# Query projections of two cross-attention layers as 2x2 block products in seven multiplications

## The chip, the core and the metric

The kernel runs on one core of one Trainium2 chip. The metric is the device time of one execution in microseconds (us), the median of several runs. A core has five engines with a queue each: PE (TensorE, the matrix engine), DVE (VectorE), ACT (ScalarE), POOL (GpSimd) and SP (SyncE, here only an issuer of transfers). They run side by side and wait for one another by semaphores.

## The reference

A trunk of two residual layers over 1024 tokens of width 1024, everything in fp32. Each layer has a mixer, a cross-attention into 256 memory tokens and an MLP, every one behind an RMS norm. The change touches the query product of the cross-attention, `h @ wq`, and what feeds it:

```python
def cross_attention(h, mem_n, wq, wkv, wo):
    q = (h @ wq).reshape(B, S, X_HEADS, X_HEAD_DIM)
    kv = (mem_n @ wkv).reshape(B, M, 2, X_HEADS, X_HEAD_DIM)
    s = jnp.einsum('bshd,bmhd->bhsm', q, kv[:, :, 0]).astype(jnp.float32) * X_HEAD_DIM ** -0.5
    p = jax.nn.softmax(s, axis=-1)
    o = jnp.einsum('bhsm,bmhd->bshd', p.astype(h.dtype), kv[:, :, 1]).reshape(B, S, D_MODEL)
    return o @ wo
...
        h = h + even_mixer(hn, ...)       # layer 0; odd_mixer in layer 1
        h = h + cross_attention(rms_norm(h, norm_xattn_g[l]), mem_n, xattn_wq[l], xattn_wkv[l], xattn_wo[l])
        h = h + sq_relu_mlp(rms_norm(h, norm_mlp_g[l]), mlp_w1[l], mlp_w2[l])
```

## The kernel before, in words

**Operands.** Every fp32 matrix is cut in two (`cut`, L72 and L73): ACT copies it to a rounded type (hi), and DVE subtracts that from the original (lo). A product is three matmul passes: hi by hi, lo by hi, hi by lo. Activations lie transposed, as tiles of 128 channels by 1024 tokens; most live in a pool of 44 slots of 128x1024. Weights stream through four raw buffers (`wr`) and two buffers each for hi and lo (`wh`, `wl`). `w_cut` cuts one unit ahead of its use.

**Two kinds of product.** `gemm` makes one 128x1024 output tile: 8 channel tiles by 3 passes by 2 halves, 48 matmuls of 128x512. `split_gemm` makes two output tiles by a 2x2 block product in seven multiplications instead of eight: 7 products of 12 matmuls of 128x512, 84 instead of 96. It needs weights as sums and differences of blocks (POOL, L149 to L153, in the tiles `wr` and `wt`), the operand in seven such combinations (`combine`, L247 to L250, four adds on DVE, and the class `Split`, groups 0 to 3), and it adds seven partial results: products 0 to 6 lie in banks `x`, `yz`, and `evac` takes each to one or two of the four output blocks, by an ACT copy first and by DVE adds then. Before, only the MLP uses it (m0a and m1a: first matrix, m0b and m1b: second).

**Stages.** By the names of the trace, in order: the even mixer; `X`, its output product with the residual add (`residual`, L815); `c0q`, eight query gemms (`query`, L877); the cross stage with `c0s` (scores, L904), `c0s_p` (softmax: reduce L908, four exponentials L913, row scaling L922), `c0tp` (transposes) with `c0pt` (their cut) and `c0po` (times the values); `c0o`, its output product; m0a, m0b. Then layer 1: the conv mixer, `cvo` in the place of `X`, c1q, c1s to c1po, c1o, m1a, m1b.

**Around the change.** `residual` is called for `X`, `cvo`, `c0o` and `c1o`. With `split=True` (before: `c0o` and `c1o` alone) each pair of output tiles is scaled, combined and cut into the seven parted tiles of the following `split_gemm`; the last pair's tiles are needed by that one at once. Its first pair of output tiles is therefore run with `first=True`: products 0 and 1 on the first three channel steps, then their last step, then products 3 and 2 likewise. The norm's row factors are made in two steps (`stage1`, `stage2`: a POOL power of 1.65 us, L320), which come as hooks between products. Keys and values were computed ahead into memory; `kv_get(c)` (L867) loads 2 tiles of 512 KB and cuts them, hi on ACT (L872) and lo on POOL (L873). `kv_get(0)` stands behind query 3; `score(0)` stands ahead of the last query gemm (`query(7)`), and `kv_get(1)` behind `score(1)`.

The order within each engine's queue is made by a scheduler that follows the order of the code by priority and the buffers that are free.

Of the kernel before, what the change touches and what calls it, by code (L numbers as in the profile page):

```python
# [40 lines left out]
def hybrid_trunk(ctx: ExitStack, tc: tile.TileContext, xT, memT, vecs, lams, rel, onehot, negrow, invcnt,  # L41
# [48 lines left out]
    for l in range(2):  # L90
        if l == 1:
            for j in range(KT):
                order += [(FLAT, conv_in[i * KT + j]) for i in (1, 2, 0)]
            order += [(FLAT, conv_out[n]) for n in range(KT)]
        order += [(FLAT, wq[l, n]) for n in range(KT)]
        order += [(FLAT, wo[l, n]) for n in range(KT)]
        order += [(FLAT, w1[l, 2 * p], w1[l, 2 * p + 1]) for p in range(4 * KT // 2)]
        order += [(FLAT, w2[l, c, 2 * p], w2[l, c, 2 * p + 1]) for c in range(4) for p in range(KT // 2)]
# [77 lines left out]
    class Act:  # L176
# [75 lines left out]
    def split_gemm(act, name, evac, hooks=None, first=False, tail=False):  # L252
# [16 lines left out]
        def out(i):  # L269
            for n, h in (TAIL_ADDS if tail else ADDS)[i]:  # L270
                evac(n, h, banks[(TAIL if tail else SPLIT)[i][2]], (n, h) not in seen)
                seen.add((n, h))

        for i in range(7):
            if i % 2 == 0:
                ws.append(w_next())
            for fn in (hooks or {}).get(i, ()):
                fn()
            if first and i < 4:
                if i % 2 == 1:  # L280
# [509 lines left out]
    while wait:  # L790
        tock()
    Y = Act()
    for i, _ in enumerate(fill_kv(1)):
        if i % YGAP == 0 and i // YGAP < KT:
            k = (0, 1, 2, 4, 5, 6, 7, 3)[i // YGAP]
            Y.t[k] = pair(f"Y{k}")
            cut(*Y.t[k], o_t[k] if k < 4 else y_t[k - 4])

# [16 lines left out]
    def residual(act, g_col, name, split=False):  # L815
# [4 lines left out]
        for n in range(KT):  # L820
# [10 lines left out]
            if split and n == KT - 1:  # L831
                w, ps = w_next(), psg(f"{name}_{n}")
                for h in range(2):
# [18 lines left out]
            if split and n % 2 == 1:  # L852
                tt, t4 = (slot(f"{name}_t{i}_{j}") for i in range(2))
                combine(r[0], r[1], tt, t4[:, :H])
                for g, raw in ((1, tt), (2, r[1]), (3, t4[:, :H])):
                    nx.group(g, j, raw)
            if split and n == KT - 1:
                nn.add(t[:, half(1)], 1, last=True)
            h_store(n, t, name)
        return nx, nn  # L860

    X, nrm = residual(Y, G_X[0], "X1")

    def cross(l, X, nrm, g_next, name):
        kvp = {}

        def kv_get(c):  # L867
            for cc, sh in ((c, (P, 4, M)), (2 + c, (P, 2, H))):
# [3 lines left out]
                nc.scalar.activation(kvp[cc][0], t, AF.Copy)  # L872
                nc.gpsimd.tensor_sub(kvp[cc][1], t, f32(kvp[cc][0]))  # L873

        rc = small.tile([P, KT], F32, tag="rc16", name=f"{name}_rc16")
        Q = Act()
        def query(n):  # L877
            ps = gemm(X, f"{name}q{n}", {5: nrm.stage1} if n == 0 else None)
            Q.t[n] = pair(f"{name}q{n}")
            cut(*Q.t[n], ps)  # L880
            if n == 1:
                nc.vector.tensor_scalar_mul(rc, nrm.rcol, 1.0 / 16.0)
            if n == 3:
                kv_get(0)

        for n in range(KT - 1):
            query(n)
        units = [(h, th) for h in range(4) for th in range(2)]
# [58 lines left out]
        n = len(units)  # L947
        score(0)
        query(KT - 1)
        norm_p(0)  # L950
        for u in range(n + 1):
            if u + 1 < n:
                score(u + 1)
                if u == 0:
                    kv_get(1)
            if u >= 1:
# [10 lines left out]
    def mlp(l, X, nrm, g_next, name):  # L967
# [57 lines left out]

        def merged(*hooks):
            return {i: [f for h in hooks for f in h.get(i, ())] for i in range(7)}


# [9 lines left out]

        rest, ahead = {4: [nrm.stage1], 6: [nrm.stage2]}, []  # L1040
        for p in range(2 * KT):
# [62 lines left out]
    def conv_mixer(X, nrm, g_next, name):  # L1104
        hooks = with_norm(nrm)
        Y = Act()
        for j in range(KT):
# [18 lines left out]
            nc.vector.tensor_mul(y, y, psb_)  # L1126
            Y.t[j] = pair(f"{nm}g")
            cut(*Y.t[j], y)
        return residual(Y, g_next, f"{name}o")

# [30 lines left out]
def _layout(inp):  # L1161
# [40 lines left out]
    g["conv_out"] = tiles(a["conv_w_out"][0])  # L1202
    g["wq"] = tiles(a["xattn_wq"])
    g["wkv"] = a["xattn_wkv"].reshape(2, 4, 2, P, 4, H).transpose(0, 4, 1, 3, 2, 5)
    g["wo"] = tiles(a["xattn_wo"])

    halves = [0, 2, 4, 6, 1, 3, 5, 7]
    g["w1"] = tiles(a["mlp_w1"])[..., halves, :]
    g["w2"] = tiles(a["mlp_w2"].reshape(2, 4, D, D))[..., halves, :]
    return {n: np.ascontiguousarray(v) for n, v in g.items()}  # L1210

# [17 lines left out]
```

## Time and profile before

| | before |
|---|---|
| median of 3 runs | 2615.15 us (2613.42 to 2619.64) |
| the profiled execution | 2622.43 us, span of the trace 2620.6 us |
| PE busy | 2541.0 us, 97% of the span |
| DVE, ACT, POOL busy | 1641.9 (63%), 1009.8 (39%), 694.4 us (26%) |
| mean granted PE clock | 0.99 |
| HBM | 249.91 MB read, 114.03 MB written, 139 GB/s |

The span is what the trace covers; the execution's own time is 1.8 us more. PE's ends are modelled, so a busy PE is one with matmuls queued without a gap. A matmul row's own duration (0.39 us) overlaps that of the next; the distance between starts is what one costs.

### The profile page before, as it was taken

The numbers are of one execution on the slowest core, as the hardware profiler recorded it, in microseconds if no ns is written. First come the engines' busy times: TensorE is split into PE (matmuls) and PEld (weight loads), VectorE is DVE, ScalarE is ACT, GpSimd is POOL, SyncE is SP. The second block draws the span as 40 slices with busy tenths as digits, with TensorE's granted clock in tenths as the row PEclk, the third lists the DMA queues.
The fourth block names the chain that finished last, engine by engine and source line by source line (L and its number), as shares of the span: only waits on it lengthen the run. The fifth ranks groups of instructions, "written<-read, shape, count | busy, mean of one in ns | idle before, by whom it ended". The sixth has DMA issues, their size and how long they took to land.

```text
span 2620.6 us, 29978 instructions
## 1 busy us (share of the span) xinstructions
PE 2541.0 (97%) x11618; PEld 2076.6 (79%) x11618; DVE 1641.9 (63%) x1846; ACT 1009.8 (39%) x1389; POOL 694.4 (26%) x417
## 2 busy tenths in 40 slices
PE   7999999999999999999999999999999999999997
PEld 5777778888878888777788888888887888777786
DVE  7777764325567778877773333323566777877875
ACT  4554564225443334433342111222443433433432
POOL 3222100200233334323352111111032333422334
PEclk9999999999999999999999999999999999999998
DMA  5101146311324445777742111422133344777752
GB/s 170 33 25 49 52 160 211 112 66 51 114 89 144 149 161 212 282 266 248 256 143 73 49 49 51 145 82 70 49 121 113 141 158 159 261 268 241 264 203 95
DMA packets 108430, 365.89 MB, mean 140 GB/s; under 512 B 12416, under 2 KB 14848, under 8 KB 108288
## 3 DMA queue, kind: packets, MB, share of 16 engines
q1 hardware_dynamic: 74880, 252.82, 28.7%
q10 hardware_dynamic: 33408, 111.16, 11.1%
q8 instruction: 91, 1.49, 0.2%
q14 instruction: 51, 0.42, 0.1%
HBM read 249.91 MB, written 114.03 MB: 139 GB/s over the span
## 4 chain that ended last, share of the span: by engine, by line
PE 81%; DVE 7%; issue 6%; DMA 3%; ACT 2%; SPq 0%; POOL 0%; DVEq 0%; ACTq 0%; POOLq 0%
PE m1a_x L265 7%; PE m0a_x L265 7%; PE m1a_yz L265 5%; PE m0a_yz L265 5%; PE m1b_x L265 5%; PE m0b_x L265 4%; PE m1b_yz L265 4%; PE cvo L189 3%; PE X L189 3%; PE c0o L189 3%; PE c1o L189 3%; PE m0b_yz L265 3%; PE c1q L189 3%; PE c0q L189 3%; PE qkv L189 3%
## 5 line engine op out<-in xcount | busy, mean ns | idle before, releaser
L72 ACT ACTIVATE wh<-wr 128x1024 fp32r<-128x1024 f32 (+1 forms) x310 | 301.0, 971 | 953.5 <-PE m0b_yz L265 154.9
L73 DVE TENSOR_TENSOR wl<-wr,wh 128x1024 fp32r<-128x1024 f32 (+1 forms) x310 | 361.5, 1166 | 210.6 <-ACT wh L72 209.8
L152 POOL TENSOR_TENSOR wr<-wr,wr 128x512 f32<-128x512 f32 x63 | 88.7, 1408 | 703.0 <-DVE wl L73 703.0
L73 DVE TENSOR_TENSOR wl<-wt,wh 128x1024 fp32r<-128x1024 f32 x64 | 135.7, 2120 | 4.8 <-ACT wh L72 4.6
L153 POOL TENSOR_TENSOR wr<-wr,wt 128x512 f32<-128x512 f32 x63 | 125.8, 1997 | 0.0
L150 POOL TENSOR_TENSOR wt<-wr,wt 128x512 f32<-128x512 f32 x63 | 119.9, 1904 | 4.8
L149 POOL TENSOR_TENSOR wt<-wr 128x512 f32<-128x512 f32 x63 | 90.5, 1436 | 92.0 <-issue 65.3
L72 ACT ACTIVATE wh<-wt 128x1024 fp32r<-128x1024 f32 x64 | 67.4, 1054 | 55.6 <-PE m0b_x L265 20.4
L1117 POOL TENSOR_TENSOR cv_z<-cv_z,cv_cg 128x1024 f32<-128x1024 f32 x8 | 26.2, 3276 | 175.4 <-DVE cv_z L1116 175.4
L565 ACT ACTIVATE s_p<-s,s_negm 128x128 f32<-128x128 f32 (+7 forms) x64 | 47.2, 740 | 29.1 <-DVE s_negm L564 26.1
L976 DVE SCALAR_TENSOR_TENSOR m1a_r<-m1a_r,c1o_rbc 128x1024 f32<-128x1024 f32 x32 | 52.2, 1636 | 0.9
L976 DVE SCALAR_TENSOR_TENSOR m0a_r<-m0a_r,c0o_rbc 128x1024 f32<-128x1024 f32 x32 | 52.2, 1636 | 0.9
L977 ACT ACTIVATE m1a_r<-m1a_r 128x1024 f32<-128x1024 f32 x32 | 33.9, 1061 | 42.6 <-DVE m1a_r L976 42.6
L977 ACT ACTIVATE m0a_r<-m0a_r 128x1024 f32<-128x1024 f32 x32 | 33.9, 1061 | 42.4 <-DVE m0a_r L976 42.4
L308 POOL TENSOR_TENSOR X_acc<-X_acc,X_sq 128x1024 f32<-128x1024 f32 x7 | 17.5, 2497 | 123.2 <-ACT X_sq L307 123.2
L564 DVE TENSOR_REDUCE s_negm<-s 128x1 f32<-128x128 f32 (+7 forms) x64 | 46.5, 749 | 0.2
L843 DVE TENSOR_TENSOR X1h<-X1h,X 128x1024 f32<-128x1024 f32 x8 | 9.8, 1221 | 58.0 <-PE X L189 58.0
L843 DVE TENSOR_TENSOR cvoh<-cvoh,cvo 128x1024 f32<-128x1024 f32 x8 | 9.8, 1221 | 57.3 <-PE cvo L189 57.3
L991 DVE TENSOR_TENSOR m1a_r<-m1a_r,m1a_yz 128x512 f32<-128x512 f32 x32 | 22.0, 686 | 36.6 <-PE m1a_yz L265 36.6
L991 DVE TENSOR_TENSOR m0a_r<-m0a_r,m0a_yz 128x512 f32<-128x512 f32 x32 | 22.0, 687 | 36.6 <-PE m0a_yz L265 36.6
L577 DVE SCALAR_TENSOR_TENSOR s_p<-s_p,rden,s_p 128x128 f32<-128x128 f32 (+7 forms) x32 | 36.0, 1125 | 6.4 <-ACT s_p L576 6.2
L308 POOL TENSOR_TENSOR c1o_acc<-c1o_acc,c1o_sq 128x1024 f32<-128x1024 f32 x6 | 15.5, 2588 | 91.0 <-ACT c1o_sq L307 91.0
(2717 smaller groups left out, 7986.9 us busy)
## 6 DMA issues: line engine op xcount, KB each, us to landing
wr<-in_w_dram SPq DMA_DIRECT2D x128, 512.0 KB, 3.8
m0f<-m0a_d SPq DMA_DIRECT2D x48, 512.0 KB, 5.9
m1f<-m1a_d SPq DMA_DIRECT2D x48, 512.0 KB, 6.1
wr<-in_wkv_dram SPq DMA_DIRECT2D x32, 512.0 KB, 3.5
m0a_d<-m0a_r ACTq DMA_DIRECT2D x32, 512.0 KB, 2.9
m1a_d<-m1a_r ACTq DMA_DIRECT2D x32, 512.0 KB, 2.9
wr<-in_conv_in_dram SPq DMA_DIRECT2D x24, 512.0 KB, 3.5
wr<-in_wq_dram SPq DMA_DIRECT2D x16, 512.0 KB, 3.6
```

Of the source, the lines that this page charges most:

```text
L72: nc.scalar.activation(hi, src, AF.Copy)
L73: nc.vector.tensor_sub(lo, src, f32(hi))
L149: nc.gpsimd.tensor_add(t[:, 4:], b[:, :4], b[:, 4:])
L150: nc.gpsimd.tensor_sub(t[:, :4], a[:, :4], t[:, 4:])
L152: nc.gpsimd.tensor_sub(a[:, :4], b[:, :4], a[:, :4])
L153: nc.gpsimd.tensor_add(a[:, 4:], a[:, 4:], t[:, :4])
L189: nc.tensor.matmul(ps, wt[:, k, :], act.part(k, i, h), start=(k == 0 and wt is hi and i == 0), stop=(k == ks - 1 and wt is lo))
L265: nc.tensor.matmul(banks[b], w[a][:, 4 * (i % 2) + j, :], act.part(g, s, j, c), start=(new and j == 0 and n == 0), stop=(j == nk - 1 and n ...
L564: nc.vector.tensor_reduce(s["negm"][:, m : m + 1], ps[:, :L], axis=AX.X, op=ALU.max, negate=True)
L565: nc.scalar.activation(s["pr"][m][:, :L], ps[:, :L], AF.Exp, bias=s["negm"][:, m : m + 1], accum_out=s["den"][:, m : m + 1])
L976: nc.vector.scalar_tensor_tensor(v, v, 0.0, b(), op0=ALU.max, op1=ALU.mult)
L977: nc.scalar.activation(t, t, AF.Square)
```

## The change

Six things, in both layers.

1. `query` makes two tiles with `split_gemm`: four pairs instead of eight gemms. The weights `wq` are stored with their channel tiles in the order of the halves and loaded as pairs; POOL makes the sums.
2. `X` and `cvo` are residuals with `split=True`. Their operands, the mixer outputs, take a new layout (`Halves`): hi and lo of one half of the tokens in one tile, cut in halves.
3. The last pair's group 2, group 3, the norm's last add and the store of the last tile are no longer issued by `residual`: they are `X.late`, hooks at products 2, 3 and 4 of the next stage's first pair (query or MLP). `residual` cuts one more weight unit in its last product instead. The MLP's `stage1` moves from product 4 to 5.
4. Keys and values: lo on DVE instead of POOL; `kv_get(0)`, `kv_get(1)` and `score(0)` are hooks at products 2, 4 and 6 of the last query pair.
5. All `evac` calls of `split_gemm` are scheduled with high priority, in the MLP too.
6. The weights' host layout follows.

```diff
-        order += [(FLAT, wq[l, n]) for n in range(KT)]
+        order += [(FLAT, wq[l, 2 * p], wq[l, 2 * p + 1]) for p in range(KT // 2)]
...
+    class Halves(Act):
+        def put(self, name, k, src):
+            t = [slot(f"{name}{k}_{h}", F32R) for h in range(2)]
+            self.t[k] = t
+            for h in range(2):
+                cut(t[h][:, :H], t[h][:, H:], src[:, half(h)])
+        def part(self, k, i, h):
+            return self.t[k][h][:, i * H : (i + 1) * H]
...
         def out(i):
-            for n, h in (TAIL_ADDS if tail else ADDS)[i]:
-                evac(n, h, banks[(TAIL if tail else SPLIT)[i][2]], (n, h) not in seen)
-                seen.add((n, h))
+            with tc.high_priority():
+                for n, h in (TAIL_ADDS if tail else ADDS)[i]:
+                    evac(n, h, banks[(TAIL if tail else SPLIT)[i][2]], (n, h) not in seen)
+                    seen.add((n, h))
...
                     if h == 0:
                         nx.group(0, j, r[0])
                         nn.add(t[:, half(h)], h, last=True)
+                    else:
+                        w_cut()
...
                 combine(r[0], r[1], tt, t4[:, :H])
-                for g, raw in ((1, tt), (2, r[1]), (3, t4[:, :H])):
-                    nx.group(g, j, raw)
+                nx.group(1, j, tt)
+                if n < KT - 1:
+                    nx.group(2, j, r[1])
+                    nx.group(3, j, t4[:, :H])
             if split and n == KT - 1:
-                nn.add(t[:, half(1)], 1, last=True)
-            h_store(n, t, name)
+                nx.late = {2: [lambda: nx.group(2, j, r[1])], 3: [lambda: nn.add(t[:, half(1)], 1, last=True)],
+                           4: [lambda: nx.group(3, j, t4[:, :H]), lambda: h_store(n, t, name)]}
+            else:
+                h_store(n, t, name)
...
-    X, nrm = residual(Y, G_X[0], "X1")
+    X, nrm = residual(Y, G_X[0], "X1", split=True)
...
-                nc.gpsimd.tensor_sub(kvp[cc][1], t, f32(kvp[cc][0]))
+                nc.vector.tensor_sub(kvp[cc][1], t, f32(kvp[cc][0]))
...
-        def query(n):
-            ps = gemm(X, f"{name}q{n}", {5: nrm.stage1} if n == 0 else None)
-            Q.t[n] = pair(f"{name}q{n}")
-            cut(*Q.t[n], ps)
-            if n == 1:
-                nc.vector.tensor_scalar_mul(rc, nrm.rcol, 1.0 / 16.0)
-            if n == 3:
-                kv_get(0)
-        for n in range(KT - 1):
-            query(n)
+        def query(p, hooks):
+            r = [slot(f"{name}q{p}_r{n}") for n in range(2)]
+            for n in range(2):
+                Q.t[2 * p + n] = pair(f"{name}q{2 * p + n}")
+            def evac(n, h, ps, new):
+                q, d = [x[:, half(h)] for x in Q.t[2 * p + n]], r[n][:, half(h)]
+                if (n, h) == (1, 0):
+                    cut(*q, ps)
+                elif new:
+                    nc.scalar.activation(d, ps, AF.Copy)
+                else:
+                    nc.vector.tensor_add(d, d, ps)
+                    if (n, h) == (1, 1):
+                        cut(*q, d)
+                    elif h == 1:
+                        cut(*Q.t[2 * p], r[0])
+            split_gemm(X, f"{name}q{p}", evac, hooks, first=(p == 0))
+        def divide():
+            nc.vector.tensor_scalar_mul(rc, nrm.rcol, 1.0 / 16.0)
...
-        score(0)
-        query(KT - 1)
+        for p, hooks in enumerate((merged(X.late, {5: [nrm.stage1]}), {1: [divide]}, {},
+                                   {2: [lambda: kv_get(0)], 4: [lambda: kv_get(1)], 6: [lambda: score(0)]})):
+            query(p, hooks)
         norm_p(0)
         for u in range(n + 1):
             if u + 1 < n:
                 score(u + 1)
-                if u == 0:
-                    kv_get(1)
...
-        rest, ahead = {4: [nrm.stage1], 6: [nrm.stage2]}, []
+        rest, ahead = merged(X.late, {5: [nrm.stage1], 6: [nrm.stage2]}), []
...
-        return residual(Y, g_next, f"{name}o")
+        return residual(Y, g_next, f"{name}o", split=True)
```

**Where it moves instructions.** First place: ACT at the border of c0o and m0a, before the change. `c0o_x_3h` are the last pair's cuts of groups 1 and 2 (out of `c0o_t` and `c0o_r`), `c0o_x_3` that of group 3, `m0a_r<-m0a_x` the copy that takes product 0, and then product 2, out of bank x.

```order
L72 ACTIVATE c0o_x_3h<-c0o_t_3_6059 128x1024
L72 ACTIVATE c0o_x_3h<-c0o_r_1_5924 128x1024
L72 ACTIVATE wh_2_6115<-wr_0_5778 128x1024
L72 ACTIVATE c0o_x_3_6073<-c0o_t_3_6060 128x512
L307 ACTIVATE c0o_sq<-c0oh_5839 128x512
L987 ACTIVATE m0a_r_6081<-m0a_x 128x512
L987 ACTIVATE m0a_r_6082<-m0a_x 128x512
```

The same place with the change:

```order
L72 ACTIVATE c0o_x_3h<-c0o_t_3_6203 128x1024
L1021 ACTIVATE m0a_r_6213<-m0a_x 128x512
L72 ACTIVATE wh_2_6243<-wr_0_5918 128x1024
L72 ACTIVATE c0o_x_3h<-c0o_r_1_6064 128x1024
L323 ACTIVATE c0o_sq<-c0oh_5979 128x512
L1021 ACTIVATE m0a_r_6214<-m0a_x 128x512
```

The copy out of bank x has moved from behind five instructions of the residual to behind one. DVE at the border of X and the first query pair, with the change (`X_x_3l` are the last pair's lo parts, `c0q_r` the first pair's sums):

```order
L262 TENSOR_TENSOR X_t_3_4423<-X_r_0_4282,X_t_3_4422 128x512
L73 TENSOR_TENSOR X_x_3l<-X_t_3_4422,X_x_3h 128x1024
L912 TENSOR_TENSOR c0q_r_4433<-c0q_r_4433,c0q_yz 128x512
L73 TENSOR_TENSOR wl_2_4468<-wr_0_4137,wh_2_4467 128x1024
L73 TENSOR_TENSOR X_x_3l<-X_r_1_4283,X_x_3h 128x1024
L324 TENSOR_TENSOR X_acc<-X_acc,X_sq 128x512
```

Before, DVE had at that border:

```order
L843 TENSOR_TENSOR X1h_4144<-X1h_4144,X_7_4282 128x1024
L73 TENSOR_TENSOR wl_0_4343<-wr_0_4083,wh_0_4342 128x1024
L76 SCALAR_TENSOR_TENSOR X_x7l<-X1h_4144,vec,X_x7h 128x1024
L317 TENSOR_REDUCE X_ms<-X_n_4379 128x4
L317 TENSOR_REDUCE X_ms<-X_n_4385 128x4
```

So combinations, three more cuts and the first sum of the queries have come between the last add and the norm's reduces. Last place: DVE at the end of the queries, before.

```order
L73 TENSOR_TENSOR c0q6l<-c0q_4729,c0q6h 128x1024
L908 TENSOR_REDUCE c0s_mx<-c0s_4782 128x4
L909 TENSOR_TENSOR c0s_mx<-c0s_mx,c_rc_4341 128x4
L920 RECIPROCAL c0rd_4875<-c0s_den 128x4
L922 TENSOR_SCALAR c0s_p<-c0s_p,c0rd_4875 128x256 x4
L73 TENSOR_TENSOR wl_0_5472<-wr_0_4609,wh_0_5471 128x1024
L73 TENSOR_TENSOR c0q7l<-c0q_4822,c0q7h 128x1024
```

With the change:

```order
L912 TENSOR_TENSOR c0q_r_4843<-c0q_r_4843,c0q_yz 128x512
L73 TENSOR_TENSOR wl_0_4974<-wr_0_4786,wh_0_4973 128x1024
L895 TENSOR_TENSOR c0kv1l<-c0kv_4931,c0kv1h 128x1024
L943 TENSOR_REDUCE c0s_mx<-c0s_4979 128x4
L944 TENSOR_TENSOR c0s_mx<-c0s_mx,c_rc_4432 128x4
L895 TENSOR_TENSOR c0kv3l<-c0kv_4937,c0kv3h 128x1024
L73 TENSOR_TENSOR wl_0_5612<-wr_0_4788,wh_0_5611 128x1024
L73 TENSOR_TENSOR c0q7l<-c0q_x,c0q7h 128x512
L73 TENSOR_TENSOR c0q7l<-c0q_r_4844,c0q7h 128x512
L943 TENSOR_REDUCE c0s_mx<-c0s_5033 128x4
L73 TENSOR_TENSOR c0q6l<-c0q_r_4843,c0q6h 128x1024
```

The cuts of keys and values (`c0kv1l`, `c0kv3l`; `c0kv0l` and `c0kv2l` a little earlier) were POOL's; the first softmax (reduce, reciprocal, scaling) stood ahead of query 7's cut, and its scaling now comes behind the cuts of queries 6 and 7.

## Rows read from the trace of the kernel before

**Rows 1.** The page, busy time of PE and shares of the others

```profile
PE 2541.0 (97%) x11618; PEld 2076.6 (79%) x11618; DVE 1641.9 (63%) x1846; ACT 1009.8 (39%) x1389; POOL 694.4 (26%) x417
```

**Rows 2.** Windows by stage: us, busy of PE, PEld, DVE, ACT, POOL, clock, DMA

```profile
424.00:511.00 87.00, 87.00 (x386) 72.08 (x385) 28.19 (x25) 24.72 (x24) 14.93 (x6) 1.00 0.41 142
511.00:593.00 82.00, 81.69 (x376) 68.12 (x375) 21.41 (x25) 18.70 (x25) 8.98 (x4) 1.00 0.20 67
593.00:653.00 60.00, 54.81 (x332) 48.36 (x332) 37.23 (x70) 29.74 (x77) 4.75 (x2) 0.94 0.16 53
653.00:754.00 101.00, 98.14 (x439) 80.71 (x437) 62.94 (x64) 48.65 (x67) 25.28 (x12) 1.00 0.29 99
...
1733.00:1815.00 82.00, 81.69 (x376) 68.14 (x375) 21.39 (x25) 18.70 (x25) 8.98 (x4) 1.00 0.21 68
```

**Rows 3.** The chain that ended last, query stage: start, us, what

```profile
515.86 68.94 PE c0q L189 x304
```

**Rows 4.** Windows, same columns: twelve later pairs of m0a

```profile
832.00:1058.00 226.00, 226.00 (x995) 185.57 (x994) 176.43 (x170) 91.10 (x111) 83.09 (x47) 1.00 0.49 175
```

**Rows 5.** Timeline of PE at the start of m0a and of m1a: start, us

```profile
754.36 0.80 PE L265 MATMUL m0a_x<-c0o_x_0h,wh 128*128 128x512 f32 x1 [3.16 <-ACT m0a_r L987]
...
763.15 0.48 PE L265 MATMUL m0a_x<-c0o_x_0h,wh 128*128 128x512 f32 x1
...
1976.36 0.80 PE L265 MATMUL m1a_x<-c1o_x_0h,wh 128*128 128x512 f32 x1 [3.15 <-ACT m1a_r L987]
```

**Rows 6.** The chain that ended last, same place: start, us, what

```profile
754.36 4.21 PE m0a_x L265 x9
758.57 3.03 PE m0a_yz L265 x9
```

**Rows 7.** Timeline of ACT, same place

```profile
749.00 1.06 ACT L72 ACTIVATE c0o_x_3h<-c0o_t 128x1024 fp32r<-128x1024 f32 x1 [1.28 <-DVE c0o_t L248]
750.79 1.06 ACT L72 ACTIVATE c0o_x_3h<-c0o_r 128x1024 fp32r<-128x1024 f32 x1 [0.73 <-DVE c0o_r L249]
...
753.74 0.57 ACT L987 ACTIVATE m0a_r<-m0a_x 128x512 f32<-128x512 f32 x1
```

**Rows 8.** Timeline of DVE, same place

```profile
748.28 0.68 DVE L248 TENSOR_TENSOR c0o_t<-c0o_t,c0o_r 128x512 f32<-128x512 f32 x1
748.88 1.79 DVE L249 TENSOR_TENSOR c0o_r<-c0o_r 128x512 f32<-128x512 f32 x1
...
752.28 1.21 DVE L73 TENSOR_TENSOR c0o_x_3l<-c0o_t,c0o_x_3h 128x1024 fp32r<-128x1024 f32 x1
```

**Rows 9.** Timeline of POOL, same place

```profile
748.50 1.63 POOL L149 TENSOR_TENSOR wt<-wr 128x512 f32<-128x512 f32 x1 [5.25 <-issue]
...
765.04 1.65 POOL L320 TENSOR_TENSOR c0o_rcol<-c0o_ms,mhalf 128x8 f32<-128x8 f32 x1 [13.24 <-DVE c0o_ms L319]
```

**Rows 10.** Timeline of PE, a wait in m0b

```profile
1071.23 0.51 PE L265 MATMUL m0b_x<-m0A_3l,wh 128*128 128x512 f32 x1 [1.58 <-DVE m0A_3l L73]
```

**Rows 11.** Timeline of PE, cross stage of layer 0

```profile
588.41 0.70 PE L189 MATMUL c0q<-X_x0h,wh 128*128 128x512 f32 x2 [0.31 <-DVE c0q6l L73]
...
614.99 0.80 PE L943 MATMUL c0po<-c0pt0l,c0kv2h 128*128 128x512 f32 x1 [4.58 <-DVE c0pt0l L73]
```

**Rows 12.** The chain that ended last, same place: start, us, what

```profile
614.99 5.06 PE c0po L943 x11
```

**Rows 13.** Timeline of DVE, same place: row scaling of scores 0 and 1

```profile
592.23 1.14 DVE L922 TENSOR_SCALAR c0s_p<-c0s_p,c0rd 128x256 f32<-128x256 f32 x4
...
607.60 4.81 DVE L922 TENSOR_SCALAR c0s_p<-c0s_p,c0rd 128x256 f32<-128x256 f32 x2
```

**Rows 14.** Timeline of POOL, same place

```profile
607.51 2.40 POOL L873 TENSOR_TENSOR c0kv1l<-c0kv,c0kv1h 128x1024 fp32r<-128x1024 f32 x1 [44.42 <-ACT c0kv1h L872]
```

**Rows 15.** Groups of instructions by line, 511 to 653 us: busy, mean ns

```profile
L908 DVE TENSOR_REDUCE c0s_mx<-c0s 128x4 f32<-128x1024 f32 x8 | 9.7, 1215 | 0.0
...
L913 ACT ACTIVATE c0s_p<-c0s,c0s_mx,c_rc 128x256 f32<-128x256 f32 x30 | 16.5, 562 | 21.3 <-DVE c0s_mx L909 21.3
```

More of the change, by code (lines that the diff above doesn't have):

```diff
@@ L289, in split_gemm, with merged @@
                 out(i)
+    def merged(*hooks):
+        return {i: [f for h in hooks for f in h.get(i, ())] for i in range(7)}
     class Norm:
@@ L791, in hybrid_trunk @@
         tock()
-    Y = Act()
+    Y = Halves()
     for i, _ in enumerate(fill_kv(1)):
@@ L795, in hybrid_trunk @@
             k = (0, 1, 2, 4, 5, 6, 7, 3)[i // YGAP]
-            Y.t[k] = pair(f"Y{k}")
-            cut(*Y.t[k], o_t[k] if k < 4 else y_t[k - 4])
+            Y.put("Y", k, o_t[k] if k < 4 else y_t[k - 4])
     hd = {n: xT[n] for n in range(KT)}
@@ L1024, in ready @@
             return run
-        def merged(*hooks):
-            return {i: [f for h in hooks for f in h.get(i, ())] for i in range(7)}
         def prepare(c, left):
@@ L1105, in conv_mixer @@
         hooks = with_norm(nrm)
-        Y = Act()
+        Y = Halves()
         for j in range(KT):
@@ L1126, in conv_mixer @@
             nc.vector.tensor_mul(y, y, psb_)
-            Y.t[j] = pair(f"{nm}g")
-            cut(*Y.t[j], y)
-        return residual(Y, g_next, f"{name}o")
+            Y.put(f"{nm}g", j, y)
+        return residual(Y, g_next, f"{name}o", split=True)
     X, nrm = cross(0, X, nrm, G_MLP[0], "c0")
@@ L1202, in _layout @@
     g["conv_out"] = tiles(a["conv_w_out"][0])
-    g["wq"] = tiles(a["xattn_wq"])
     g["wkv"] = a["xattn_wkv"].reshape(2, 4, 2, P, 4, H).transpose(0, 4, 1, 3, 2, 5)
@@ L1207, in _layout @@
     halves = [0, 2, 4, 6, 1, 3, 5, 7]
+    g["wq"] = tiles(a["xattn_wq"])[..., halves, :]
     g["w1"] = tiles(a["mlp_w1"])[..., halves, :]
     g["w2"] = tiles(a["mlp_w2"].reshape(2, 4, D, D))[..., halves, :]
-    return {n: np.ascontiguousarray(v) for n, v in g.items()}
+    names = ("xT memT vecs lams rel onehot negrow invcnt w_qk0 w_in w_out pool_w conv_in conv_out "
+             "wq wkv wo w1 w2").split()
+    return {n: np.ascontiguousarray(g[n]) for n in names}
 def kernel(**inputs):
```

## The prediction

> **What bounds the kernel now.** I read the page first. PE is busy 97% of the span and no other engine comes near [rows 1], so the time is PE's work plus the places where PE stands. Then the windows by stage, to see where each kind of time is. While the queries run, PE is busy 81.69 of 82 us in either layer, and DVE, ACT and POOL are mostly idle (21.41, 18.70 and 8.98 us); the output product ahead of them has no gap at all, 87.00 of 87.00 [rows 2]. The stage of the scores is different: PE idles 60 - 54.81 = 5.19 us and its mean clock is 0.94 [rows 2]. Third, the chain: in the query stage it is PE alone, 304 matmuls in 68.94 us, or 0.2268 us each [rows 3]. Last, the timelines at the borders, since the change moves these. PE stands 3.16 us at the start of m0a for an ACT copy and 3.15 us in m1a [rows 5], then runs its first 18 matmuls in 4.21 + 3.03 = 7.24 us [rows 6], where 18 x 0.2268 = 4.08 would do. So a stall of 3.16 us costs as much again: those matmuls run for the most part at half of the clock, 1.2 GHz for 2.4. A wait of 1.58 us in m0b [rows 10] is followed by matmuls at the full rate.
>
> **The change part by part.** Against the profiled execution, 2622.43 us, which is 7.3 us above the median of 2615.15.
>
> *Queries.* Eight gemms of 48 matmuls become four pairs of 84: 384 - 336 = 48 fewer per layer, 48 x 0.2268 = 10.89 us, for both layers **-21.8 us**, all of it on the path, as PE is the chain [rows 3]. It holds only if a pair runs without waits. What m0a's later pairs show is the nearest: PE 226.00 us busy of 226.00 with DVE at 176.43 and POOL at 83.09 [rows 4], that is 14.9 and 7.0 us of each 19.05. A query pair has the same weight cuts and POOL sums, but fewer DVE instructions: three adds of 0.68, 2.6 us of query cuts (1.21 for 1024 columns, half that for 512) and 4.4 us of weight cuts, 9.0 in all. I cost the steady pairs, all six per layer but for the first and the last, whose borders follow, at nothing; DVE's 10 idle us per pair hide them. Without that cover see the last rival.
>
> *X and cvo split.* DVE and ACT get scalings, combinations and cuts; c0o does the same today and PE is busy 98.14 of its 101 us, with a part of the score stage's tail in it [rows 2]. DVE goes from 28.19 towards 62.94 us; the stage is 87 long. Nothing.
>
> *First query pair, a new border.* At this border PE has no wait now. With the change it is a border like c0o to m0a. Bounds: 0 and what m0a pays, 3.16 + 3.16 + 0.2 = 6.5 us [rows 5, 6]. The deferral helps: the copy out of bank x no longer stands behind the cut of the last pair's group 2. It stands behind a cut of 1.06 us that starts 0.1 us after the combination [rows 7, 8]. But product 3 then waits for the sum of the yz bank on DVE, which stands behind the cut of group 1's lo part, 1.21 us [rows 8], and that behind combinations that a POOL sum beside them stretched from 0.68 to 1.79 us [rows 8, 9]. I replay this with these durations: 1.6 us before product 3, 0.5 for a weight cut behind the norm's power of 1.65 us [rows 9], 0.3 of smaller waits: 2.4 us. It is nearer to the 1.58 us that keeps the clock than to 3.16. **+2.4 per layer, +4.8.**
>
> *First pair of m0a and m1a.* The copy at 753.74 [rows 7] can start at about 750.2, behind the first of the two cuts, so the 3.16 us wait and the slow matmuls (3.16 us) go. Back come the 1.6 us before product 3 and 0.7 us at the norm, whose last sum and first step are later: -6.32 + 1.6 + 0.7 = -4.0, which I take as **-3.8 per layer, -7.6**, for 0.2 of hand-over. Bounds: -6.3 and 0. By the replay product 4 starts at 759.4 where it starts at 763.15 now [rows 5].
>
> *Scores.* Now: PE stands 4.58 us before the first value product, and 11 matmuls take 5.06 us where 11 x 0.2268 = 2.49 would do [rows 11, 12], so 2.57 more. The DVE cause: two row scalings take 4.81 us [rows 13] for 2 x 0.285 by the earlier four in 1.14, while POOL cuts keys and values for 2.40 us each [rows 14]; 4.24 us lost. With those cuts on DVE and earlier, this loss goes, and with it up to 4.24 + 2.57 = 6.8 us. But query 7's 10.88 us no longer cover the first softmax. Its chain from the end of score 0: product 6 (12 x 0.2268 = 2.72), ACT cuts of queries 7 and 6 (0.57 + 0.57 + 1.06 = 2.2), four exponentials (4 x 0.56 = 2.2) [rows 15], scaling 1.14: 8.3 us, beside 2.72 of product 6 and 24 matmuls of half the length for score 1, 24 x 0.1134 = 2.7, on PE; 2.9 us stay open. With the second reduce of 1.2 us [rows 15] and hand-overs it may be 4.5, and then the slow matmuls (2.57) stay: 7.1. Between 2.9 and 7.1 I take the middle, 5.0: -6.8 + 5.0 = **-1.8 per layer, -3.6**; bounds -3.9 and +0.3.
>
> What moves of the transfers: each layer's keys and values are the same four loads of 512 KB. The second two come two products ahead of score 0 instead of behind score 1; on SP they stand behind two weight loads of the output product, and ACT's next weight cut needs product 6 anyway. Nothing.
>
> *High priority and m0b.* The adds come a row or two earlier, not the cuts that PE waits for [rows 10]. 0, bounds of 1.3 either way per layer.
>
> Sum: -21.8 + 4.8 - 7.6 - 3.6 = -28.2. 2622.43 - 28.2 = 2594.2; against the median, **2587.0 us**.
>
> **A rule against the change.** Row scalings that take 2.4 us where 0.285 is usual, just while a POOL subtraction runs [rows 13, 14], show that DVE loses nearly all of a POOL instruction's time. The Trainium skill says so too (page "SBUF — State Buffer", section "SBUF: two separate sides"): the two share a pair of ports by an exclusive lock, the loser blocked for the whole instruction. By that rule alone, with every POOL sum of 1.7 us in the way of an add that PE waits for, the eight pairs would lose 8 x 7 = 56 us and the sum be +28; by [rows 4], where POOL does as much beside a busier DVE, nothing. I go by the rows.
>
> **The rivals.**
> *A: the first query pairs fall to half clock.* The stall before product 3 is over some 3 us, as at m0a now, and each pair pays 6.5 us for 2.4: +8.2, **2595.2 us**. For it: the combination beside a POOL sum took 1.79 us for 0.68 [rows 8]. Against it: the copy goes first now.
> *B: m0a and m1a keep their loss* because the wait moves to product 3 and stays over 3 us: +7.6, **2594.6**. With A, **2602.8**. For it: the same DVE queue decides.
> *C: both borders and the scores come out at their good ends*: 2587.0 - 4.8 - 5.0 - 4.2 = **2573**.
> *D: slower.* In every one of the eight query pairs one product waits over 3 us for an add or a weight cut blocked by a POOL sum, and the clock halves behind it: 6.3 us x 8 = 50, so +22 for -28.2: **2637**. It decides from 28.2/8 = 3.5 us lost per pair. Against it: the twelve pairs without a gap [rows 4].
> *E: the products saved turn into waits* (a slot of the pool that X's parted tiles hold, 28 for 16, comes free late, or the parting of X ends late): some 20 us back, **2606 to 2615**. The matmuls do go, 48 per layer; for a wait of this size no row speaks.
>
> **How the numbers follow.** The forecast has 0.53, its own range 2579 to 2594; A alone 0.15, B alone 0.11, A and B 0.06, C 0.07, D 0.03, E 0.05. A measurement of this kernel tells 0.3% (7.8 us) from no change, so faster means below 2607.3: all but D and E's slower part, 0.92; within 0.3%: 0.05; slower, above 2623: 0.03. The range goes from just under C's 2573, 2572, to just over A and B together, 2604; the unknown costs' bounds added up would reach 2610 (21.8 less 13, 0.6 and 2.6), which all need to come out badly at once, and 0.1 beyond the range covers that.
>
> **What would show it.** In the new profile: query stages of some 76 us of PE with no wait in pairs 1 and 2; a wait of 1 to 2.5 us before product 3 of c0q and of m0a, no run of matmuls at twice the distance behind them; no 3.16 us wait for an ACT copy; row scalings at 0.285; one wait of 3 to 5 us for the first softmax in each cross stage. Waits over 3 us in the first pairs mean A or B. A gap in each query pair, or DVE adds over 2 us beside POOL sums, means D and a wrong forecast. Any gap in X or cvo means E.

## The result, and the profile after

The changed kernel takes 2589.61 us (median of 4 runs, 2588.04 to 2590.47) against 2615.82 us of the kernel before in the same job (4 runs, 2613.42 to 2619.64): a ratio of 0.9898, 95% interval 0.9881 to 0.9915, so 22 to 31 us less, 26.2 by the medians. The forecast was 2587.0. The profiled execution takes 2590.47 us with a span of 2588.7; that of before had 2622.43 and 2620.6. The two traces lie 31.9 us apart, more than the medians, because the profiled execution of before lay above its median. What follows accounts for the 31.9 us.

The page, busy time of PE; the row of before is in [rows 1].

```profile
PE 2513.6 (97%) x11522; PEld 2053.3 (79%) x11522; DVE 1739.8 (67%) x1972; ACT 1069.1 (41%) x1503; POOL 729.2 (28%) x439
```

PE has 96 fewer matmuls, 48 per layer, and 27.4 us less busy time. Windows of the changed kernel, with the columns of [rows 2]: X; c0q from the end of its first pair (which runs to 530) over pairs 1 and 2 into pair 3; the stage of the scores; m0a.

```profile
424.00:502.00 78.00, 78.00 (x346) 64.59 (x345) 44.98 (x39) 33.18 (x40) 17.46 (x8) 1.00 0.42 148
523.00:583.00 60.00, 60.00 (x267) 49.63 (x267) 34.35 (x37) 24.63 (x33) 20.06 (x11) 1.00 0.24 76
584.00:635.00 51.00, 47.91 (x314) 43.50 (x313) 35.65 (x72) 31.32 (x83) 0.00 (x0) 0.97 0.20 69
...
727.00:1043.00 316.00, 314.22 (x1386) 257.06 (x1386) 241.95 (x237) 128.69 (x159) 114.46 (x66) 1.00 0.45 159
```

X and the later query pairs have no gap on PE, though DVE now works there for more than half of the time. The new border, X to the first query pair, and that of c0o and m0a have one wait each (timeline of PE):

```profile
517.18 0.50 PE L277 MATMUL c0q_yz<-X_x_0h,wh 128*128 128x512 f32 x1 [1.55 <-DVE c0q_r L912]
...
741.87 0.50 PE L277 MATMUL m0a_yz<-c0o_x_0h,wh 128*128 128x512 f32 x1 [1.55 <-DVE m0a_r L1025]
```

Both are the first matmul of product 3. They answer to [rows 5]: the 3.16 us wait for an ACT copy is gone. The timelines of ACT, DVE and POOL at the first border show why ([rows 7 to 9] for the same place in c0o):

```profile
512.03 1.06 ACT L72 ACTIVATE X_x_3h<-X_t 128x1024 fp32r<-128x1024 f32 x1 [1.29 <-DVE X_t L260]
513.21 0.60 ACT L910 ACTIVATE c0q_r<-c0q_x 128x512 f32<-128x512 f32 x1
```

```profile
511.92 1.78 DVE L261 TENSOR_TENSOR X_r<-X_r 128x512 f32<-128x512 f32 x1
...
515.32 1.21 DVE L73 TENSOR_TENSOR X_x_3l<-X_t,X_x_3h 128x1024 fp32r<-128x1024 f32 x1
516.46 0.67 DVE L912 TENSOR_TENSOR c0q_r<-c0q_r,c0q_yz 128x512 f32<-128x512 f32 x1
```

```profile
511.53 1.62 POOL L149 TENSOR_TENSOR wt<-wr 128x512 f32<-128x512 f32 x1 [5.26 <-issue]
```

The copy out of bank x follows the first cut at once. The add that product 3 waits for ends a chain on DVE: two combinations of 1.78 and 1.77 us beside POOL sums, then a cut, then the add. At the score border (timeline of PE; before: [rows 11, 12]):

```profile
595.51 0.39 PE L939 MATMUL c0s<-c0kv0h,c0q2h 128*128 128x256 f32 x1 [2.19 <-ACT c0s_p L948]
...
596.75 2.03 PE L965 MATMUL c0tp<-ident,c0s_p 128*128 128x128 f32 x8 [0.73 <-DVE c0s_p L957]
...
599.00 0.41 PE L939 MATMUL c0s<-c0kv0l,c0q3h 128*128 128x256 f32 x1
599.21 0.41 PE L939 MATMUL c0s<-c0kv0h,c0q3l 128*128 128x256 f32 x1
```

Two waits of 2.19 and 0.73 us take the place of one of 4.58 us. Behind them matmuls of 256 columns start 0.21 us apart where 0.12 is usual: half of the clock again. The granted clock is 0.83 from 595 to 605 us, and 0.66 at the same place in layer 1 (1801 to 1811 us), where the slow stretch is longer. The row scalings are at their usual 0.285 us each, and the last cuts of the queries come ahead of the exponentials (timelines of ACT and DVE):

```profile
592.23 1.05 ACT L72 ACTIVATE c0q6h<-c0q_r 128x1024 fp32r<-128x1024 f32 x1
593.18 0.55 ACT L948 ACTIVATE c0s_p<-c0s,c0s_mx,c_rc 128x256 f32<-128x256 f32 x1
```

```profile
594.83 1.22 DVE L73 TENSOR_TENSOR c0q6l<-c0q_r,c0q6h 128x1024 fp32r<-128x1024 f32 x1
...
596.25 1.14 DVE L957 TENSOR_SCALAR c0s_p<-c0s_p,c0rd 128x256 f32<-128x256 f32 x4
```

The 31.9 us by stage, each from its first matmul to that of the next; the fourth column is what the prediction had for the stages.

| stage | before | after | difference | predicted |
|---|---|---|---|---|
| X to m0a (queries, first pair, scores) | 318.57 | 306.28 | -12.29 | -10.3 |
| cvo to m1a | 318.56 | 307.25 | -11.31 | -10.3 |
| m0a | 319.49 | 315.88 | -3.61 | -3.8 |
| m1a | 319.79 | 315.91 | -3.88 | -3.8 |
| m0b | 321.02 | 321.04 | 0.0 | 0 |
| m1b, to its last matmul's start | 321.46 | 320.65 | -0.8 | 0 |
| the conv mixer, cv0c to cvo | 262.93 | 262.93 | 0 | 0 |

### The profile page after: what moved, and what is told of

Read it like the earlier page. It is cut to its first block, busy times and chain, and to the rows that moved or that the text cites. A ratio compares the mean times of both kernels' runs of the same rounds, so it can differ in the third digit from the quotient of the medians.

```text
span 2588.7 us, 30102 instructions
## 1 busy us (share of the span) xinstructions
PE 2513.6 (97%) x11522; PEld 2053.3 (79%) x11522; DVE 1739.8 (67%) x1972; ACT 1069.1 (41%) x1503; POOL 729.2 (28%) x439
## 3 DMA queue, kind: packets, MB, share of 16 engines
q10 hardware_dynamic: 33408, 111.16, 11.3%
## 5 line engine op out<-in xcount | busy, mean ns | idle before, releaser
L152 POOL TENSOR_TENSOR wr<-wr,wr 128x512 f32<-128x512 f32 x71 | 104.4, 1470 | 762.8 <-DVE wl L73 758.6
L73 DVE TENSOR_TENSOR wl<-wt,wh 128x1024 fp32r<-128x1024 f32 x72 | 148.4, 2062 | 7.3 <-ACT wh L72 7.1
L153 POOL TENSOR_TENSOR wr<-wr,wt 128x512 f32<-128x512 f32 x71 | 142.0, 2000 | 0.0
L150 POOL TENSOR_TENSOR wt<-wr,wt 128x512 f32<-128x512 f32 x71 | 135.5, 1909 | 5.3
L149 POOL TENSOR_TENSOR wt<-wr 128x512 f32<-128x512 f32 x71 | 101.4, 1428 | 122.7 <-issue 75.0
L72 ACT ACTIVATE wh<-wt 128x1024 fp32r<-128x1024 f32 x72 | 75.9, 1055 | 62.7 <-PE m1b_x L277 18.7
L1148 POOL TENSOR_TENSOR cv_z<-cv_z,cv_cg 128x1024 f32<-128x1024 f32 x8 | 26.2, 3275 | 175.4 <-DVE cv_z L1147 175.4
L201 PE MATMUL X<-Y,wh 128*128 128x512 f32 x256 | 69.8, 390 | 0.0
L201 PEld LDWEIGHTS X<-Y,wh 128*128 128x128 f32 x256 | 48.0, 188 | 10.2 <-DVE X1h L851 0.3
L324 POOL TENSOR_TENSOR c0o_acc<-c0o_acc,c0o_sq 128x1024 f32<-128x1024 f32 x6 | 15.5, 2589 | 118.6 <-ACT c0o_sq L323 118.6
```

Source lines behind the costliest of these rows:

```text
L72: nc.scalar.activation(hi, src, AF.Copy)
L73: nc.vector.tensor_sub(lo, src, f32(hi))
L149: nc.gpsimd.tensor_add(t[:, 4:], b[:, :4], b[:, 4:])
L150: nc.gpsimd.tensor_sub(t[:, :4], a[:, :4], t[:, 4:])
L152: nc.gpsimd.tensor_sub(a[:, :4], b[:, :4], a[:, :4])
L153: nc.gpsimd.tensor_add(a[:, 4:], a[:, 4:], t[:, :4])
```

## The experiments

The theory after the result: the queries give 10.9 us per layer, the deferral gives 3.7 us at each MLP and keeps the new border at 2.2 us, and the score border gives some 3 us because the subtractions of keys and values no longer stand where they did. Open were what moved the copy (deferral or priority), whether the engine or the place of the subtractions counted, and whether product 3's wait is one for data. The kernel before was run beside each job; its median was 2619.19 us in the first (e1 to e4), 2617.52 in the second (e5 to e8) and 2618.14 in the third (e9, e10).

**e1: no priority.** `out` calls `evac` without it:

```diff
-            with tc.high_priority():
-                for n, h in (TAIL_ADDS if tail else ADDS)[i]:
+            for n, h in (TAIL_ADDS if tail else ADDS)[i]:
```

> The changed kernel without the high priority on the sums of the block product. Theory: the deferral of the residual's last groups, not the priority, moved the copy out of bank x at the four borders (its queues stand there in the same order with and without the priority), so the first pairs keep their one wait of 1.55 us, and m0b changes by at most 1.3 us per layer: within 3 us of the changed kernel's 2589.6. Rival: the priority did it; then 3.16 us waits and slow matmuls come back at four borders and the time goes up by some 16 us.

Measured: 2586.83 us, ratio 0.9876 (0.9859 to 0.9893), whose interval overlaps that of the change. Waits of PE between 495 and 760 us (in total, times, longest):

```profile
PE c0s L938 <- ACT c0s_p L947: 2.3, 2, 2.2
PE c0q_yz L277 <- DVE c0q_r L911: 1.6, 1, 1.6
PE m0a_yz L277 <- DVE m0a_r L1024: 1.6, 1, 1.6
```

The same waits within 0.2 us, and m0b takes 320.85 us for 321.04. No gain from the priority can be measured. The changed kernel was not run again in this first job; e1 stands for it below, since its stages are the same within 0.7 us.

**e2: no deferral.** The residual issues its last groups itself:

```diff
-                nx.group(1, j, tt)
-                if n < KT - 1:
-                    nx.group(2, j, r[1])
-                    nx.group(3, j, t4[:, :H])
+                for g, raw in ((1, tt), (2, r[1]), (3, t4[:, :H])):
+                    nx.group(g, j, raw)
...
-                nx.late = {2: ...
+                nn.add(t[:, half(1)], 1, last=True)
+                nx.late = {}
```

> The changed kernel with groups 2 and 3, the last norm sum and the last store issued by the residual again, the priority kept. Theory: at each of the four borders the copy out of bank x stands behind five instructions of the residual again; a 3.16 us wait with slow matmuls, about 6.4 us, in the place of 1.55 us and 0.7 of small waits: +4.2 us per border, +17 us in all, 2606. Rival: the borders' gain came from the priority; then the time stays within 3 us of 2589.6.

Measured: 2605.46 us, ratio 0.9947 (0.9928 to 0.9966), 18.6 us above e1. The timeline of PE:

```profile
516.78 0.51 PE L277 MATMUL c0q_x<-X_x_0h,wh 128*128 128x512 f32 x1 [3.16 <-ACT c0q_r L906]
...
744.52 0.50 PE L277 MATMUL m0a_x<-c0o_x_0h,wh 128*128 128x512 f32 x1 [3.15 <-ACT m0a_r L1017]
...
747.17 0.79 PE L277 MATMUL m0a_yz<-c0o_x_0h,wh 128*128 128x512 f32 x1 [0.82 <-DVE m0a_r L1021]
747.76 0.63 PE L277 MATMUL m0a_yz<-c0o_x_0l,wh 128*128 128x512 f32 x1
```

The wait of [rows 5] is back, at the new border too, and with it slow matmuls (0.42 us apart behind it at c0q, and from 747.76 on at m0a). By stages the borders cost 3.4, 5.4, 5.4 and 4.5 us more (c0q, m0a, c1q, m1a), 18.7 in all. The deferral, not the priority, moved the copy; without it the change would be worth some 14 us.

**e3: keys and values on POOL again, at the new place.**

```diff
-                nc.vector.tensor_sub(kvp[cc][1], t, f32(kvp[cc][0]))
+                nc.gpsimd.tensor_sub(kvp[cc][1], t, f32(kvp[cc][0]))
```

> The changed kernel with the lo parts of keys and values on POOL again, at their new place in the last query pair. Theory: it was the engine: POOL subtractions of 2.4 us block DVE, so reduces, cuts or scalings near them take 2.4 us again and the score border loses some 4 us more per layer, +8 us. Rival: it was the place: behind score 1 the subtractions met the row scalings, in the last query pair they meet instructions that PE does not wait for; then the time is within 2 us of 2589.6.

Measured: 2584.11 us, ratio 0.9865 (0.9847 to 0.9883): not slower, as the theory had it, but 2.7 us below e1. The two ratio intervals overlap, so the stage has to decide. From the first query matmul to the first of c0o it is 130.22 us for the change's 132.71, in layer 1 130.23 for 133.63 (132.09 and 133.38 in e1). That is 5.0 us less than e1 for both layers; the mixer ahead of X, which the edit does not touch, took 2.3 us longer in this trace, so that less shows in the whole time. At the score border PE keeps one wait, for the exponentials, and no slow matmuls behind it (timeline of PE, then of POOL and DVE):

```profile
599.87 0.39 PE L939 MATMUL c0s<-c0kv0h,c0q2h 128*128 128x256 f32 x1 [1.66 <-ACT c0s_p L948]
```

```profile
587.98 2.41 POOL L895 TENSOR_TENSOR c0kv3l<-c0kv,c0kv3h 128x1024 fp32r<-128x1024 f32 x1 [2.73 <-ACT c0kv3h L894]
```

```profile
588.26 1.23 DVE L943 TENSOR_REDUCE c0s_mx<-c0s 128x4 f32<-128x1024 f32 x1 [0.78 <-PE c0s L939]
589.52 0.89 DVE L944 TENSOR_TENSOR c0s_mx<-c0s_mx,c_rc 128x4 f32<-128x4 f32 x1
```

The POOL subtraction costs DVE 0.7 us there (0.16 is usual for this instruction, which ends here when the subtraction does), against four cuts of 1.22 us each that DVE is spared. The reduce of the scores, which reads them out of PSUM, ran beside the same subtraction in its usual 1.23 us. Both expectations missed: the engine does count, with the other sign, by 2.5 and 3.4 us against the change and 1.9 and 3.1 against e1.

**e9 and e10: engine and place apart, in the kernel before.** e9 makes the same replacement of `gpsimd` by `vector` in the kernel before, at the old place. e10 leaves POOL and moves the place:

```diff
-            if n == 3:
-                kv_get(0)
+            if n in (3, 5):
+                kv_get(n // 4)
...
-                if u == 0:
-                    kv_get(1)
```

> The kernel before with the lo parts of keys and values on DVE, at their old place behind score 1. If the engine is what cost, the two row scalings of 2.4 us are 0.285 again and, with the two subtractions of 1.2 us that DVE takes over, the wait of 4.58 us shrinks by 2 to 4 us and the slow matmuls go: 3 to 6 us per layer, 2605 to 2611 against 2617.5. If it is the place (any work on keys and values between the scaling and the cut of the transposed probabilities), the wait stays over 3 us and the time moves by less than 3 us.

> The kernel before with the second keys and values fetched and cut behind query 5, on POOL as before. If the place is what cost, the wait of 4.58 us and the slow matmuls behind it go: 6 to 7 us per layer, some 2604. If the engine matters wherever it stands, or the first softmax is the bound, the wait stays over 3 us and the time within 3 us of 2617.5.

Measured: e9 2609.82 us, ratio 0.9971 (0.9961 to 0.9981); e10 2604.43 us, ratio 0.9952 (0.9935 to 0.9969). From the first query matmul to the first of c0o the layers take 139.57 and 139.59 us before, 136.43 and 136.41 in e9, 132.53 and 132.30 in e10. In e9 the scalings are quick, but DVE's own cuts of keys and values stand behind them, the last just ahead of the cut that PE waits for (timelines of DVE and PE):

```profile
608.08 1.13 DVE L922 TENSOR_SCALAR c0s_p<-c0s_p,c0rd 128x256 f32<-128x256 f32 x4
...
611.67 1.23 DVE L873 TENSOR_TENSOR c0kv3l<-c0kv,c0kv3h 128x1024 fp32r<-128x1024 f32 x1
612.81 1.28 DVE L73 TENSOR_TENSOR c0pt0l<-c0tp,c0pt0h 128x512 fp32r<-128x512 f32 x2
```

```profile
613.55 0.50 PE L943 MATMUL c0po<-c0pt0l,c0kv2h 128*128 128x512 f32 x1 [2.57 <-DVE c0pt0l L73]
613.89 0.43 PE L943 MATMUL c0po<-c0pt0h,c0kv2l 128*128 128x512 f32 x1
614.12 0.62 PE L943 MATMUL c0po<-c0pt0h,c0kv2h 128*128 128x512 f32 x1
614.54 0.63 PE L943 MATMUL c0po<-c0pt0l,c0kv2h 128*128 128x512 f32 x1
```

The time of e9 is where the theory of the engine had it, but the slow matmuls, which were to go, stayed. In e10 the waits of PE between 500 and 670 us are these, and no others of over 0.1 us:

```profile
PE c0s L904 <- ACT c0s_p L913: 0.8, 2, 0.5
PE c0q L189 <- DVE c0q6l L73: 0.3, 1, 0.3
```

So the place alone is worth 7.0 and 7.3 us per layer, the engine alone 3.1 and 3.2: DVE at the old place is better than POOL there, and at the early place of the changed kernel POOL is the better one (e3). DVE at the early place of the kernel before was not run. One call moved, without any block product, gives 13.7 us by the medians, half of what the whole change gives.

**e5: the deferral and the priority alone**, in the kernel before (diff as in the change, parts 3 and 5).

> The kernel before with the deferral of the residual's last groups and the priority alone; queries, X, cvo, keys and values as before. Theory: this part is worth what the first pairs of m0a and m1a show, 3.6 to 3.8 us per layer, and nothing else moves: 7.4 us below the kernel before, so that about 24 us of the whole change are the queries and the score border. Rival: the 3.16 us wait went for another reason (the operand or the queries' own arrangement), then the time is that of the kernel before.

Measured: 2611.81 us, ratio 0.9979 (0.997 to 0.9988), 5.7 us less than before where 7.4 was expected, which lies within the ratio's interval. m0a takes 315.70 us and m1a 315.96, 3.8 us less each; X to m0a stays at 318.1 and cvo to m1a at 318.6. Waits of PE:

```profile
PE c0po L954 <- DVE c0pt0l L73: 4.7, 1, 4.7
PE m0a_yz L265 <- DVE m0a_r L1002: 1.6, 1, 1.6
```

The first pair of m0a shows the 1.6 us wait and the scores the old 4.7: the parts are independent.

**e4: banks y and z as two tiles.** The add that product 3 waits for reads bank y; product 3 writes bank z. Both are halves of one PSUM tile. With the edit each takes one of the two buffers of 128x1024 that successive pairs used in turn, and fills half of it, so a pair no longer has a second buffer to go to.

```diff
-        x, yz = psb(f"{name}_x", tag="f"), psg(f"{name}_yz")
-        banks = x, yz[:, :H], yz[:, H:]
+        x, y, z = psb(f"{name}_x", tag="f"), psg(f"{name}_y"), psg(f"{name}_z")
+        banks = x, y[:, :H], z[:, :H]
```

> The changed kernel with banks y and z of the block product as two tiles of PSUM instead of the halves of one. Theory: product 3 writes z and has no data to wait for in the first pairs; it waited for the DVE add that reads y because both are one tile. Then the wait of 1.55 us goes at four borders, -6 us, and the waits of 1.4 us of product 3 in m0b and m1b (three of 1.4 and two of 0.5 us per layer) go too, up to -17 us in all: 2573 to 2584. Rival: the add is late for the next product as well, so that the wait moves to product 4 or 5 and the time stays at 2589.6.

Measured: 2578.02 us, ratio 0.9845 (0.9825 to 0.9865), 8.8 us below e1. Waits of PE between 495 and 1040 us:

```profile
PE c0s L939 <- ACT c0s_p L948: 2.4, 2, 2.2
PE c0tp L965 <- DVE c0s_p L957: 0.7, 1, 0.7
PE c0o_b L345 <- POOL c0o_rcol L336: 0.4, 1, 0.4
```

The wait of product 3 is gone, and nothing of it came back later in the pair: c0q to the first score is 80.21 us for 82.09, m0a 314.09 for 315.88. It was no wait for data, and it went although the edit took the second buffer away. In m0b product 3's waits, 5.1 us in all, are gone as well, but a part of that comes back (waits of PE, 1030 to 1364 us):

```profile
PE m0b_x L277 <- DVE m0b0h L1095: 3.2, 3, 1.7
PE m0b_x L277 <- DVE wl L73: 2.3, 3, 1.3
PE m0b_x L277 <- ACT wh L72: 1.6, 3, 0.5
```

The first two rows stood in the changed kernel too, at 3.3 and 2.5 us; the third, for the weight cuts on ACT, is new. m0b and m1b take 317.67 and 317.87 us, 3 us less each.

**e6: e3 and e4 together.**

> The changed kernel with two tiles for banks y and z, and the lo parts of keys and values on POOL. If the two effects are independent (1.85 us at each of four borders and 3 us in m0b and in m1b; 2.5 to 3.4 us in each score stage), it lies 19 us below the changed kernel, about 2570. Rival: at the score border the two overlap (the scores take the same PSUM buffers), then it stays within 3 us of the kernel with two tiles alone, 2575 to 2578.

Measured: 2570.07 us, ratio 0.9813 (0.9799 to 0.9826): 47 us below the kernel before and, by the ratios, some 22 below the changed one. From the first query matmul to the first of c0o 128.58 and 128.36 us for the change's 132.71 and 133.63; the effects add up. No kernel that was run is faster.

**e7 and e8: score 0 a product earlier**, in e6 and in the changed kernel.

```diff
-  4: [lambda: kv_get(1)], 6: [lambda: score(0)]
+  4: [lambda: kv_get(1)], 5: [lambda: score(0)]
```

> As the one before, with score 0 ahead of product 5 instead of product 6. Theory: what PE waits for at the score border is the first softmax, with one more product (2.7 us) ahead of it as cover; the wait of 1.66 us for an exponential goes and each score stage gains 1.5 to 2.5 us: some 4 us less than the one before. Rival: the cuts of queries 6 and 7, which need the last products, end last; then nothing changes.

> The changed kernel with score 0 ahead of product 5 only. Theory: the two waits of 2.19 and 0.73 us and the slow matmuls behind them shrink by the 2.7 us of cover: 2 to 5 us per layer, 2580 to 2586. Rival: with keys and values on DVE its queue (cuts of values, weights and queries between the reduce and the row scaling) decides, and the waits stay as they are.

Measured: e7 2571.55 us, ratio 0.9818 (0.9804 to 0.9831), no gain over e6; e8 2590.10 us, ratio 0.9889 (0.9875 to 0.9902), none over the change. Waits of PE in e8:

```profile
PE c0s L939 <- ACT c0s_p L948: 2.4, 2, 2.2
...
PE c0tp L965 <- DVE c0s_p L957: 0.7, 1, 0.7
```

They are those of the change to the tenth, as e8's rival had it. Its reason, DVE's queue, holds for the second wait: DVE works without a gap from 591.51 us to the end of the row scaling. For the first wait it is ACT's queue: the exponentials still stand behind the cuts of query 7 and, all but the first, behind that of query 6, and these cuts need the last products. In e7 the wait for an exponential shrinks from 1.66 to 0.42 us, and 0.86 us before the transposes come in its place. The POOL subtraction now meets a cut of query 7 (timelines of DVE and POOL), which takes 2.57 us for 0.68:

```profile
586.22 2.57 DVE L73 TENSOR_TENSOR c0q7l<-c0q_r,c0q7h 128x512 fp32r<-128x512 f32 x1 [0.24 <-ACT c0q7h L72]
```

```profile
585.75 2.49 POOL L895 TENSOR_TENSOR c0kv3l<-c0kv,c0kv3h 128x1024 fp32r<-128x1024 f32 x1 [4.84 <-ACT c0kv3h L894]
```

From the first query matmul to the first of c0o e7 gains 0.6 and 0.4 us over e6, less than the 1.5 to 2.5 expected; m0b, with a stretch of slow matmuls in this trace, takes 2.3 us more than in e6.

## Why the prediction was right, point by point

*Queries, -21.8.* Right: 96 matmuls fewer, and the later pairs run without a gap (60.00 of 60.00) with DVE at 34.35 us of 60, 10.9 per pair where 9.0 was counted (the end of the first pair and the last pair's first cuts of keys and values lie in that window). No run has the block products of the queries alone; the 10.9 us per layer are read from the count of matmuls and from these windows.

*X and cvo, 0.* Right: 78.00 of 78.00.

*First query pair, +2.4.* Right: beyond 0.2268 us from one matmul to the next, this border loses some 2.2 us, 1.72 of it before product 3, where 1.6 was forecast. The mechanism that was replayed is the one in the rows. What the prediction took for given, that product 3 needs the add, is not so: e4 shows that it waits for the other half of its tile.

*m0a and m1a, -3.8.* Right: -3.6 and -3.9, and alone, in e5, -3.8 each. It is the deferral (e2), not the priority (e1).

*Scores, -1.8.* The sign was right and the size too small. What is left of the -12.3 and -11.3 us after 10.9 for the queries and 2.2 for the first pair is -3.6 and -2.6 per layer. The first half of the term, 6.8 us for the loss that goes, fits e10, where the place alone is worth 7.0 and 7.3. By difference the second half, the first softmax laid open, cost some 3.4 and 4.7 us, for the 5.0 taken between 2.9 and 7.1. The waits, 2.19 + 0.73 = 2.9 us, came out at the lower end; the slow matmuls behind them, which the lower end left out, did come, and for longer in layer 1, which is the 1 us between the layers. What failed is a part of the reason, "with those cuts on DVE and earlier, this loss goes": earlier is what counts (e10, with POOL), and DVE at the new place costs 2.5 and 3.4 us (e3).

*The rule against the change.* At the new border the combinations take 1.78 us beside POOL sums and 0.68 us otherwise [rows 8]. In the steady pairs, with as many POOL sums, PE waits for nothing; the cost is at the borders, where the add stands behind these combinations. The Trainium skill (page "SBUF — State Buffer", section "SBUF: two separate sides") states an exclusive lock on a pair of ports that DVE and POOL share, held for a whole instruction. The stretched rows, 1.78 us for 0.68, agree with it; the loss of 56 us that it could have meant did not come.

*Rivals.* A and B did not come: no first pair waits over 1.55 us. e2 brings their waits of over 3 us back at all four borders, though for the copy and not for the add of product 3, and lies 18.6 us above e1, where the prediction put A and B at 15.8. C did not come: both borders and the scores stayed short of their good ends. D did not come: no gap in a later pair. E did not come: no gap in X or cvo.

The sum was -28.2 for a difference of -31.9 between the traces, of which 2.7 are the scores and 0.8 m1b. By the medians the difference is -26.2, and the ratio's interval, 22 to 31 us, holds the -28.2 but not quite the 31.9 of these two traces.

## What to carry to other kernels

A border between stages is worth a replay of its own, with durations from a like border: here its order in the queues of ACT and DVE set 18 us, nearly as much as the saved multiplications. Before a wait is accepted, ask whether the matmul reads or overwrites what the releaser touches; here it did not, and two tiles instead of the halves of one removed that wait at four borders. When a helper engine disturbs a critical stretch, first move its work in time; changing the engine puts the work into a queue that may be just as critical.

## What the runs showed of the hardware

The prediction took the loss of the clock to lie between waits of 1.58 and 3.16 us. The runs show that the length of the wait alone does not decide. Behind one wait of 1.66 us (e3) the matmuls kept the 2.4 GHz level. Behind one of 2.57 us (e9) they went to 0.42 us from start to start, the 1.2 GHz level, and behind two of 2.19 and 0.73 us close together (the changed kernel) to 0.21 us for 256 columns. But behind one of 1.94 us, in m0b of e7, they went to 0.42 us too, and behind one of 3.15 us, at the start of m0a in e10, they did not. In m1a of that same execution the like wait was followed by the slow level (timelines of PE, e7 and then e10):

```profile
1067.19 0.47 PE L277 MATMUL m0b_x<-m0A_0h,wh 128*128 128x512 f32 x1 [1.94 <-DVE m0b0h L1095]
...
1068.35 0.63 PE L277 MATMUL m0b_x<-m0A_1l,wh 128*128 128x512 f32 x1
1068.77 0.63 PE L277 MATMUL m0b_x<-m0A_1h,wl 128*128 128x512 f32 x1
```

```profile
746.13 0.50 PE L265 MATMUL m0a_x<-c0o_x_0h,wh 128*128 128x512 f32 x1 [3.15 <-ACT m0a_r L985]
...
1959.16 0.50 PE L265 MATMUL m1a_x<-c1o_x_0h,wh 128*128 128x512 f32 x1 [3.15 <-ACT m1a_r L985]
...
1960.46 0.63 PE L265 MATMUL m1a_x<-c1o_x_1l,wh 128*128 128x512 f32 x1
1960.89 0.63 PE L265 MATMUL m1a_x<-c1o_x_1h,wl 128*128 128x512 f32 x1
```

The granted clock in e10 is 1.00 from 741 to 757 us and 0.89 from 1955 to 1970 us. So a stall of 3.16 us costs as much again where [rows 5] were read, but not each time: m0a takes 317.89 us in e10 for 319.49 in the kernel before, behind the same wait. Nor does the slow level begin with the first matmul behind a wait: in e9 the first starts are still 0.34 and 0.23 us apart, only then 0.42. Why it begins where it does was not tried.

A POOL subtraction can stretch even a DVE instruction on 128x4 elements: 0.89 us for 0.16 in e3. On the row scalings (2.4 us for 0.285 [rows 13, 14]), the combinations (1.78 for 0.68) and a cut of query 7 (2.57 for 0.68 in e7) it was more; the reduce out of PSUM beside the same subtraction in e3 kept its 1.23 us.
